# Layer 1 of a two-layer trunk: whole-block weight scaling and lower halves on GpSimd

## The chip, the cores and the metric

The kernel runs on one core of one Trainium2 chip. Its engines are PE (TensorE, matrix products), DVE (VectorE), ACT (ScalarE) and POOL (GpSimd); SP (SyncE) issues the transfers between HBM and SBUF, the on-chip memory. PSUM is the memory that PE writes its products to. Each engine works off its own queue in order and waits at semaphores for the others. The metric is the time of one execution on the device in microseconds (us). One execution was also recorded by the profiler; times inside it count from the span's start.

## The reference

A trunk of two layers over 1024 tokens of width 1024, in float32. Layer 0 is a native-sparse-attention mixer, layer 1 a "forgetting" attention, and each is followed by a gated ConvFFN. Only layer 1 matters here:

```python
h  = rms_norm(x, attn_norm[1])
hs = rms_norm(x, kv_norm) @ w_kv_shared            # keys, values, 12 forget gates
k_sh, v_sh = hs[..., :768], hs[..., 768:1536]      # 12 heads of 64 each
log_f = log_sigmoid(hs[..., 1536:] + b_fgate)
dcum  = cumsum(log_f, axis=1)
q, q_mem = h @ b_w_in[0]                           # 12 heads, 4 memory heads
s = q k^T / 8 + dcum[t] - dcum[s]                  # causal softmax, times v
x = x + concat(o_mix, o_mem) @ w_o[1]              # output projection
x = x + conv_ffn(rms_norm(x, ffn_norm[1]))
```

`rms_norm(x, g)` scales each of the 1024 columns by a factor of `g`. The kernel multiplies these factors into the weights: row d of a weight matrix is multiplied by g[d].

## The kernel before

Every float32 product is made of three matmuls: an operand is cut into an upper half (`hi`, rounded by a copy on ACT) and a lower half (`lo` = source minus `hi`, a subtraction), and `mm3` (L241 to L243) multiplies hi by hi, hi by lo and lo by hi. `split` (L162 to L169) makes the two halves: ACT copies at L165, and DVE subtracts at L166, or POOL, if `low` names it.

Layer 1 begins with the value projection and the forget gates: `layer1_v` fills PSUM tiles for 8 blocks of 128 tokens, in two passes of 390 columns, and its results `sv` are split on ACT and DVE and stored by SP. `forget` (L1386 and on) then takes the log-sigmoid of the 12 gates of all tokens, a tile `lsg` of 128x96: L1394 and L1395 on ACT, then a chain of 15 DVE instructions, L1396 to L1405, of which all but L1404 read what the one ahead of them wrote. PE waits for its result `r` at L1410, the matmul that starts the running sum, and stands still until it comes, because the matmuls of the second pass of `layer1_v` that follow are behind it in PE's queue.

After that `layer1_attn` runs `attention()`: the key and query projections (14 blocks of 128 output columns, in the order k0, q0, q6, k1, q1, k2, q2, q7, k3, q3, k4, q4, k5, q5) are filler between the steps of the attention units. Each block's weights are 128 partitions x 8 row groups x 128 columns. `proj` calls `load_block` with step 8, and that calls `load_rows` (L274 to L287): one transfer into a tile `wr` (three buffers), then for each of the 8 row groups one ACT instruction at L285 (upper half `wh`, 128x128, scaled by that group's factor `gc`) and one DVE instruction at L286 (lower half `wl` = `wr` times `gc` minus `wh`). `wh` and `wl` have four buffers each. Which instruction of the interleaved work comes where in an engine's queue is the scheduler's choice; a transfer into `wr` waits until the block that held the buffer has been read.

Towards the end of the attention `operand()` (L580 to L589) makes the 16 operands `hT` of the output projection: a transfer of two halves from HBM into `wr` (L587), their sum on POOL (L588), the upper half on ACT (L165) and the lower half on DVE (L166). Some are made while attention steps still run, the rest after the last one. The weights `w_o` of the output projection go through the same `wr` buffers (`load_rows` without factors, loads at L274). Other names below: `ps` are scores, normalised by DVE at L474 (a scaling from SBUF to SBUF); L518 makes the lower half of the transposed scores `pt` from PSUM; `st` are projected keys and queries.

Of the kernel before, what the change touches and what calls it, by code (L numbers as in the profile page):

```python
# [13 lines left out]
ALU = mybir.AluOpType  # L14
# [4 lines left out]
P = 128  # L19
# [3 lines left out]
KT = D // P  # L23
# [103 lines left out]
class Trunk:  # L127
# [422 lines left out]
    def attention(self, ap, l, od, units, work, spare, lead=4, lag=2, lead_work=2):  # L550
# [4 lines left out]
        steps, items, users = [], [], {}  # L555
# [23 lines left out]
        later, halves, whole, oT = {}, [], [], []  # L579

        def operand():

            if not oT:
                oT.extend(self.hpair() for _ in range(2))
            c, kt = whole.pop(0)
            raw = self.wraw([P, 2, CH])
            self.nc.sync.dma_start(raw, od[c][:, kt * P:(kt + 1) * P, :].rearrange("s p q -> p s q"))  # L587
            self.nc.gpsimd.tensor_tensor(raw[:, 0], raw[:, 0], raw[:, 1], ALU.add)  # L588
            self.split(raw[:, 0], oT[c][0][:, kt, :], oT[c][1][:, kt, :])  # L589

        def after(k, slot, f):
            later.setdefault((k, slot), []).append(f)
# [36 lines left out]
        for k in range(first, len(steps) + lag + 4):  # L629
            st = steps[k] if 0 <= k < len(steps) else None  # L630
            run(k, "max")
            if st:
                self.turn_p(ap, st)
                self.upper_p(ap, st)
            run(k, "exp")
            if st:
                self.lower_p(st)
            run(k, "norm")
            while items and items[0]["at"] <= k:
                begin(k, items.pop(0))  # L640
            if k < 0 and lead_work and items:
                for _ in range(lead_work):
                    if work:
                        advance()
            if st and k < n_fill:
                owed += max(total, 0) / (n_fill - k)
                while owed >= 1 and work:
                    owed -= 1
                    advance()
            if 0 <= k - lag < len(steps):  # L650
                for part in range(len(steps[k - lag]["t"])):
                    self.value(steps[k - lag], part)
                if steps[k - lag]["end"]:
                    finish(k, steps[k - lag]["u"])
            if not work and whole and k % 4 == 0:
                operand()
            if k == units[-1]["start"]:
                w_o = self.load_block(self.a["w_o"][l], [(0, CH)])
        while whole:
            operand()  # L660
# [769 lines left out]
    def layer1_attn(self, h, gc):  # L1430
        od = self.o_dram(1)
        wkv, wq = self.a["w_kv_shared"], self.a["b_w_in"][0]
        self.n_pt, self.n_q = 3, 1
        with self.tc.tile_pool(name="l1a", bufs=1) as ap:
            def proj(w, g, dst, m, scale):
                at = self.load_block(w, [(m * P, P)], g, 8)
                yield from self.plain_proj(ap, h, lambda kt: at(kt, 0, P), dst, m, scale)

            def k(m):
                return ("k", m), 9, proj(wkv, gc[:, 0:8], self.kd1, m, None)  # L1440

            def q(m):
                return ("q", m), 9, proj(wq, gc[:, 8:16], self.qd1, m, QSC)
            work = [k(0), q(0), q(6), k(1), q(1), k(2), q(2), q(7)]
            for m in range(3, 6):
                work += [k(m), q(m)]
            fox = list(self.units1(ap))
            mem = list(self.mem_units(ap, self.qd1[:, NH * HD:, :], self.mem[1], [("ps0", 1280, 2)] * 2, lambda h: ("q", 6 + h // 2), "dve"))
            units = []
            for i in range(6):  # L1450
                units += fox[4 * i:4 * i + 4] + (mem[2 * i:2 * i + 2] if i < 4 else [])
            return self.attention(ap, 1, od, units, work, 5)
# [521 lines left out]
```

## Time and profile before

| | us |
|---|---|
| median of 3 runs | 2570.05 (2568.84 to 2573.27) |
| the profiled execution | 2571.99 |
| its span, first to last instruction | 2570.2 |
| PE busy | 2465.7 (96%) |
| DVE busy | 1822.5 (71%) |
| ACT busy | 1339.1 (52%) |
| POOL busy | 794.5 (31%) |
| mean granted TensorE clock | 0.987 |

In the chain of work that ended last PE has 76% of the span, DVE 6%, ACT and DMA 4% each and POOL 3%. POOL does hardly anything in layer 1's attention: in the slices of the page from about 1400 to 1800 us its digit is 0. What counts is therefore where PE stands still in layer 1, and who ends that wait: the timelines list start, duration, engine, line and operation, and in square brackets how long the engine sat idle before and what released it.

### The profile page before, as it was taken

How to read it: one execution, taken by the hardware profiler on the slowest of the kernel's cores; microseconds unless marked ns; L12 is line 12 of the kernel's file. 1: busy time of each engine (PE TensorE's matmuls, PEld its weight loads, DVE VectorE, ACT ScalarE, POOL GpSimd, SP SyncE). 2: the span in 40 equal slices, each digit the busy share in tenths (PEclk: the TensorE clock that was granted, in tenths of full speed). 3: DMA queues.
4: the chain of work that ended last, by engine and by line, in shares of the span. 5: the costliest groups of instructions: out<-in, count | busy, mean ns of one | idle time of the engine just before them, and what ended most of it. 6: DMA issues, size and time to landing. Idle time of an engine off the chain costs nothing.

```text
span 2570.2 us, 35647 instructions
## 1 busy us (share of the span) xinstructions
PE 2465.7 (96%) x12306; PEld 2062.9 (80%) x12306; DVE 1822.5 (71%) x3074; ACT 1339.1 (52%) x2553; POOL 794.5 (31%) x714
## 2 busy tenths in 40 slices
PE   7889999988999999999999999999999999999998
PEld 7778888766778888888889988887777888888886
DVE  5638787676377778779665467878476777788765
ACT  5328787677145444444454356767234444445443
POOL 1335555476124554540000000000234555451000
PEclk9999999999999999999999999999999999999999
DMA  8473234243422332349334466665632233338533
GB/s 250 137 212 92 83 103 116 87 140 108 157 74 90 111 107 91 115 143 324 92 126 149 141 188 188 194 186 167 218 108 78 91 115 103 99 107 297 171 98 115
DMA packets 302700, 357.68 MB, mean 139 GB/s; under 512 B 37960, under 2 KB 183224, under 8 KB 302520
## 3 DMA queue, kind: packets, MB, share of 16 engines
q1 hardware_dynamic: 302520, 355.41, 44.1%
q8 instruction: 97, 1.59, 0.3%
q14 instruction: 83, 0.68, 0.1%
HBM read 245.55 MB, written 109.78 MB: 138 GB/s over the span
## 4 chain that ended last, share of the span: by engine, by line
PE 76%; DVE 6%; ACT 4%; DMA 4%; POOL 3%; issue 2%; SPq 0%; POOLq 0%; ACTq 0%; DVEq 0%
PE psa L241 12%; PE psa L242 12%; PE psa L243 12%; PE psb L241 9%; PE psb L243 9%; PE psb L242 9%; PE psa L384 5%; PE psb L504 4%; PE psb L528 4%; DVE pt L518 1%; ACT pt L515 1%; DVE ps L414 1%; ACT ps L427 1%; DMA wr<-o 1%; DMA wr<-in_w_up_dram 1%
## 5 line engine op out<-in xcount | busy, mean ns | idle before, releaser
L165 ACT ACTIVATE wh<-wr 128x512 fp32r<-128x512 f32 (+2 forms) x240 | 182.0, 760 | 314.1 <-PE psb L243 148.4
L1748 DVE SCALAR_TENSOR_TENSOR v<-u,cw,v 128x1023 f32<-128x1023 f32 (+1 forms) x176 | 273.1, 1552 | 68.8 <-ACT v L1746 68.5
L166 DVE TENSOR_TENSOR wl<-wr,wh 128x512 fp32r<-128x512 f32 (+2 forms) x232 | 223.2, 964 | 120.9 <-ACT wh L165 120.3
L518 DVE TENSOR_TENSOR pt<-psb,pt 128x512 fp32r<-128x512 f32 (+2 forms) x380 | 243.7, 659 | 71.3 <-ACT pt L515 69.7
L1746 ACT ACTIVATE v<-u,cw 128x1024 f32<-128x1024 f32 x88 | 109.6, 1246 | 309.9 <-DVE u L1735 283.2
L515 ACT ACTIVATE pt<-psb 128x512 fp32r<-128x512 f32 (+2 forms) x380 | 212.0, 575 | 111.7 <-PE psb L504 76.3
L528 PE MATMUL psb<-pt,vv 128*128 128x512 f32 (+2 forms) x864 | 245.5, 362 | 11.8 <-DVE pt L518 6.3
L241 PE MATMUL psa<-hT,wh 128*128 128x512 f32 x560 | 218.5, 391 | 5.3 <-DVE u L1709 5.3
L243 PE MATMUL psa<-hT,wl 128*128 128x512 f32 x560 | 218.3, 390 | 0.2 <-DVE wl L166 0.2
L242 PE MATMUL psa<-hT,wh 128*128 128x512 f32 x560 | 218.1, 390 | 0.0
L384 PE MATMUL psa<-kk,qq 128*128 128x512 f32 (+4 forms) x792 | 180.5, 347 | 23.9 <-DMA qq<-qd 12.4
L205 POOL TENSOR_TENSOR rs<-ss,consts 128x1 f32<-128x1 f32 x44 | 25.8, 588 | 573.2 <-DVE ss L203 400.7
L528 PEld LDWEIGHTS psb<-pt,vv 128*128 128x128 f32 x864 | 145.2, 191 | 33.5 <-DVE pt L518 11.9
L1650 POOL TENSOR_TENSOR ws<-wr 128x512 f32<-128x512 f32 x44 | 77.8, 1769 | 295.7 <-DMA wr<-in_w_up_dram 251.9
L414 DVE CUSTOM_DVE_ANT_0 ps<-psa,caub 128x128 f32<-128x128 f32 (+1 forms) x192 | 138.8, 750 | 41.1 <-PE psa L384 36.3
L427 ACT ACTIVATE ps<-ps,stat 128x128 f32<-128x128 f32 (+1 forms) x192 | 147.5, 771 | 30.9 <-DVE stat L414 30.7
L384 PEld LDWEIGHTS psa<-kk,qq 128*128 128x128 f32 x792 | 124.3, 195 | 45.5 <-issue 18.6
L241 PE MATMUL psb<-hT,wh 128*128 128x512 f32 x384 | 156.6, 408 | 1.1 <-ACT wh L165 0.9
L504 PE MATMUL psb<-consts,ps 128*128 128x128 f32 x928 | 149.4, 280 | 5.9 <-POOL ps L472 3.9
L243 PE MATMUL psb<-hT,wl 128*128 128x512 f32 x384 | 152.3, 397 | 0.8 <-POOL wl L166 0.6
L242 PE MATMUL psb<-hT,wh 128*128 128x512 f32 x384 | 151.2, 394 | 0.0
L588 POOL TENSOR_TENSOR wr<-wr 128x512 f32<-128x512 f32 x16 | 21.3, 1331 | 415.1 <-DMA kd<-st 248.0
(310 smaller groups left out, 6853.3 us busy)
## 6 DMA issues: line engine op xcount, KB each, us to landing
wr<-in_w_up_dram SPq DMA_DIRECT2D x88, 512.0 KB
wr<-gd SPq DMA_DIRECT2D x154, 256.0 KB
gd<-v SPq DMA_DIRECT2D x88, 256.0 KB
gd<-gs SPq DMA_DIRECT2D x66, 256.0 KB
o<-ob SPq DMA_DIRECT2D x128, 128.0 KB
wr<-o SPq DMA_DIRECT2D x32, 512.0 KB
hT<-in_w_down_dram SPq DMA_DIRECT2D x64, 256.0 KB
qd<-st SPq DMA_DIRECT2D x56, 256.0 KB
```

What stands on the lines that cost most here:

```text
L165: nc.scalar.activation(hi, src, AF.Copy)
L166: (low or nc.vector).tensor_tensor(lo, src, f32(hi), ALU.subtract)
L241: mm(out, lh, rh, start=first, stop=False, skip_group_check=more)
L242: mm(out, lh, rl, start=False, stop=False, skip_group_check=more)
L243: mm(out, ll, rh, start=False, stop=last, skip_group_check=more)
L384: nc.tensor.matmul(out, w, rhs, start=b not in banks[:i], stop=b not in banks[i + 1:])
L427: nc.scalar.activation(p, p, AF.Exp, bias=st[:, 0, ii:ii + 1], scale=-1.0, accum_out=st[:, 1, ii:ii + 1])
L504: nc.tensor.transpose(tp[0:kb, x:x + P], br["pt"][ii][:, o:o + kb], self.ident)
L515: self.nc.scalar.activation(st["hi"], st["src"], AF.Copy)
L518: self.nc.vector.tensor_tensor(st["lo"], st["src"], f32(st["hi"]), ALU.subtract)
L528: self.nc.tensor.matmul(u["o"][:, iis[0] * P:iis[0] * P + w], br["v"](j), t[:, x:x + w], start=st["begin"] and first and i == 0, stop=st[" ...
L1748: nc.vector.scalar_tensor_tensor(v[:, d:], u[:, :S - d], cw[:, tap, i:i + 1], v[:, d:], ALU.mult, ALU.add)
```

## The change

Two things in layer 1, and no others.

In `proj` the 14 weight blocks are no longer made by `load_rows`. POOL multiplies the whole block in place by the factors (one instruction of 128x1024, L1438 of the changed kernel), one ACT copy of 128x1024 makes the upper half (L165), and one POOL subtraction of 128x1024 the lower half (L166). So 112 ACT instructions become 14, and 112 DVE instructions become 28 on POOL.

In `operand()` the lower half of those operands that are made while attention steps still run (7 of the 16) moves from DVE to POOL.

```diff
@@ operand()
             self.nc.gpsimd.tensor_tensor(raw[:, 0], raw[:, 0], raw[:, 1], ALU.add)
-            self.split(raw[:, 0], oT[c][0][:, kt, :], oT[c][1][:, kt, :])
+            self.split(raw[:, 0], oT[c][0][:, kt, :], oT[c][1][:, kt, :], None, self.nc.gpsimd if k < len(steps) else None)
@@ layer1_attn()
             def proj(w, g, dst, m, scale):
-                at = self.load_block(w, [(m * P, P)], g, 8)
-                yield from self.plain_proj(ap, h, lambda kt: at(kt, 0, P), dst, m, scale)
+                raw = self.wraw([P, KT, P])
+                self.nc.sync.dma_start(raw, w[:, m * P:(m + 1) * P].rearrange("(k p) n -> p k n", p=P))
+                self.nc.gpsimd.tensor_tensor(raw, raw, g.rearrange("p (k o) -> p k o", o=1).to_broadcast([P, KT, P]), ALU.mult)
+                hi, lo = self.whl([P, KT, P])
+                self.split(raw, hi, lo, None, self.nc.gpsimd)
+                yield from self.plain_proj(ap, h, lambda kt: (hi[:, kt, :], lo[:, kt, :]), dst, m, scale)
```

The scheduler puts the instructions in another order with it. At the forget gates DVE had, before, the chain on `lsg` with one L286 of a weight block (`wl`) after nearly each step and a subtraction on `sv` at two places:

```order
L1396 TENSOR_SCALAR lsg<-lsg 128x96
L1397 RECIPROCAL lsg<-lsg 128x96
L166 TENSOR_TENSOR sv_2141_13373<-psb_13348,sv_2141_13373 128x6x64
L1398 TENSOR_TENSOR lsg<-lsg 128x96
L286 SCALAR_TENSOR_TENSOR wl_13871<-wr_13868,gc,wh_13870 128x128
L1399 TENSOR_TENSOR lsg<-lsg 128x96
L166 TENSOR_TENSOR sv_2141_13373<-psb_13348,sv_2141_13373 128x6
L1400 TENSOR_SCALAR lsg<-lsg 128x96
```

Now, on DVE at the same place:

```order
L1396 TENSOR_SCALAR lsg<-lsg 128x96
L1397 RECIPROCAL lsg<-lsg 128x96
L1398 TENSOR_TENSOR lsg<-lsg 128x96
L1399 TENSOR_TENSOR lsg<-lsg 128x96
L166 TENSOR_TENSOR sv_2141_13373<-psb_13348,sv_2141_13373 128x6x64
L1400 TENSOR_SCALAR lsg<-lsg 128x96
L1402 SCALAR_TENSOR_TENSOR lsg<-lsg 128x96
L166 TENSOR_TENSOR sv_2141_13373<-psb_13348,sv_2141_13373 128x6
L1402 SCALAR_TENSOR_TENSOR lsg<-lsg 128x96 x6
```

The weight instructions are gone from the chain, and the first `sv` subtraction stands two steps later in it.

ACT at the same place, now (`wh_13692`, `wh_13759` and `wh_13845` are the upper halves of k0, q0 and q6, `wh_13950` that of k1; before, single L285 stood between the others here, and the first `sv_2141` copy directly behind L1395):

```order
L165 ACTIVATE wh_13692<-wr_13689 128x1024
L165 ACTIVATE wh_13759<-wr_13756 128x1024
L165 ACTIVATE wh_13845<-wr_13842 128x1024
L165 ACTIVATE sv_2139_13319<-psb_13294 128x5x64
L165 ACTIVATE sv_2139_13319<-psb_13294 128x58
L1394 ACTIVATE lsg<-z 128x96
L1395 ACT_TABLE_LOAD
L1395 ACTIVATE lsg<-lsg 128x96
L165 ACTIVATE wh_13950<-wr_13947 128x1024
L165 ACTIVATE sv_2141_13373<-psb_13348 128x6x64
```

The copy of k1, which waits for POOL's multiplication of k1, now stands ahead of the `sv_2141` copy that the DVE queue waits for in the middle of the chain.

POOL's queue from the first weight block on, now (before, it had nothing between the sums of squares of the layer's norm and the first L588):

```order
L1438 TENSOR_TENSOR wr_13689<-wr_13689,gc 128x1024
L1438 TENSOR_TENSOR wr_13756<-wr_13756,gc 128x1024
L1438 TENSOR_TENSOR wr_13842<-wr_13842,gc 128x1024
L166 TENSOR_TENSOR wl_13693<-wr_13689,wh_13692 128x1024
L166 TENSOR_TENSOR wl_13760<-wr_13756,wh_13759 128x1024
L166 TENSOR_TENSOR wl_13846<-wr_13842,wh_13845 128x1024
L1438 TENSOR_TENSOR wr_13947<-wr_13947,gc 128x1024
L1438 TENSOR_TENSOR wr_14152<-wr_14152,gc 128x1024
L166 TENSOR_TENSOR wl_13951<-wr_13947,wh_13950 128x1024
L1438 TENSOR_TENSOR wr_14423<-wr_14423,gc 128x1024
L1438 TENSOR_TENSOR wr_14711<-wr_14711,gc 128x1024
L166 TENSOR_TENSOR wl_14156<-wr_14152,wh_14155 128x1024
```

The blocks are k0, q0, q6 (multiplied, then subtracted), then k1, q1, k2 and q2. Since `wr` has three buffers, the load of k1 waits for the subtraction of k0, that of q1 for the subtraction of q0, that of k2 for that of q6, and that of q2 for that of k1; SP's queue is in order, so what stands behind such a load waits with it.

At the end of the attention SP had, before, these transfers: an operand (`o` into `wr`, L587), then the four loads of the `w_o` weights, the third of which waits for a DVE instruction, the lower half of that operand:

```order
L587 DMA wr_17465<-o_1_13656 128x2x512 [waits DMAHW3_49]
L274 DMA wr_17482<-in_w_o_dram 128x2x512 [waits DMAHW4_49,DVE_49]
L274 DMA wr_17488<-in_w_o_dram 128x2x512 [waits DMAHW5_49,DVE_49]
L274 DMA wr_17494<-in_w_o_dram 128x2x512 [waits DMAHW3_49,DMAHW6_49,DVE_49,Activation_49]
L622 DMA o_1_13656<-ob_17457 64x512 [waits DMAHW7_49,Activation_49]
```

SP at the same place, now:

```order
L587 DMA wr_17283<-o_1_13656 128x2x512 [waits DMAHW3_49,Pool_49]
L274 DMA wr_17300<-in_w_o_dram 128x2x512 [waits DMAHW4_49,Pool_49]
L274 DMA wr_17306<-in_w_o_dram 128x2x512 [waits DMAHW5_49,Pool_49]
L274 DMA wr_17312<-in_w_o_dram 128x2x512 [waits DMAHW6_49,DMAHW3_49,Pool_49]
L274 DMA wr_17318<-in_w_o_dram 128x2x512 [waits DMAHW4_49,DMAHW7_49,DVE_49,Activation_49]
L622 DMA o_1_13656<-ob_17275 64x512 [waits DMAHW0_49,Activation_49]
```

Three loads now wait for POOL instead of DVE, and the fourth `w_o` load stands ahead of the store of an attention result (`ob`).

## Rows read from the trace of the kernel before

**Rows 1.** Windows: length, busy time and instructions of each engine, PEclk, DMA share, GB/s.

```profile
1420.00:1430.00 10.00, 8.14 (x46) 7.82 (x44) 8.66 (x36) 9.11 (x30) 0.00 (x0) 1.00 0.64 190
...
1460.00:1780.00 320.00, 316.33 (x1720) 265.62 (x1719) 238.70 (x594) 199.73 (x498) 5.55 (x5) 1.00 0.64 183
...
193.00:202.00 9.00, 7.92 (x28) 6.83 (x29) 4.73 (x26) 5.92 (x18) 2.64 (x3) 0.53 0.48 140
...
1431.00:1437.00 6.00, 6.00 (x21) 6.00 (x22) 2.23 (x12) 0.00 (x0) 0.00 (x0) 0.50 0.60 186
```

**Rows 2.** Waits of PE from 1380 to 1860 us: total, times, longest.

```profile
PE psb L528 <- DVE pt L518: 4.2, 8, 1.1
```

**Rows 3.** Timeline of PE: start, duration, operation, in brackets the idle time before.

```profile
1430.75 0.71 PE L1410 MATMUL psb<-lsg,tri 128*128 128x96 f32 x2 [2.60 <-issue]
...
1589.25 0.47 PE L241 MATMUL psb<-hT,wh 128*128 128x512 f32 x1
...
1830.50 0.50 PE L241 MATMUL psb<-wh,hT 128*128 128x512 f32 x1 [2.24 <-ACT hT L165]
```

**Rows 4.** Timeline of DVE in the forget gates.

```profile
1424.08 0.21 DVE L1396 TENSOR_SCALAR lsg<-lsg 128x96 f32<-128x96 f32 x1 [1.24 <-ACT lsg L1395]
1424.32 0.75 DVE L1397 RECIPROCAL lsg<-lsg 128x96 f32<-128x96 f32 x1
...
1425.40 0.25 DVE L1398 TENSOR_TENSOR lsg<-lsg 128x96 f32<-128x96 f32 x1
1425.57 0.35 DVE L286 SCALAR_TENSOR_TENSOR wl<-wr,gc,wh 128x128 fp32r<-128x128 f32 x1
...
1430.40 0.25 DVE L1405 SCALAR_TENSOR_TENSOR lsg<-lsg 128x96 f32<-128x96 f32 x1
```

**Rows 5.** Timelines of ACT and SP around the first weight blocks.

```profile
1408.55 1.13 ACT L285 ACTIVATE bh<-wr,gc 128x390 fp32r<-128x390 f32 x2 [0.48 <-DMA wr<-in_w_kv_shared_dram]
...
1423.95 0.47 ACT L165 ACTIVATE sv<-psb 128x384 fp32r<-128x384 f32 x1
...
1405.30 1.45 SPq L274 DMA_DIRECT2D wr<-in_w_kv_shared_dram  x2
...
1409.23 1.88 SPq L274 DMA_DIRECT2D wr<-in_b_w_in_dram  x2
```

**Rows 6.** Durations, by source line, by group (mean ns) and in ACT's timeline.

```profile
L286 DVE SCALAR_TENSOR_TENSOR wl<-wr,gc,wh x120: 317/344/883, 1374.2 to 1666.7; 128x128 fp32r<-128x128 f32 x112, 128x390 fp32r<-128x390 f32 x8
...
L1187 POOL TENSOR_TENSOR wl<-wr,wh x2: 2392/2402/2411, 168.2 to 358.0; 128x1024 fp32r<-128x1024 f32 x2
...
L470 POOL TENSOR_TENSOR pm<-pm,stat 128x1024 f32<-128x1024 f32 x8 | 15.2, 1896 | 0.3
...
1791.67 1.05 ACT L165 ACTIVATE wh<-wr 128x1024 fp32r<-128x1024 f32 x1
```

**Rows 7.** Timelines of DVE and POOL where the two meet, and once where they don't.

```profile
1642.87 1.29 POOL L588 TENSOR_TENSOR wr<-wr 128x512 f32<-128x512 f32 x1 [247.98 <-DMA kd<-st]
...
1643.43 1.15 DVE L286 SCALAR_TENSOR_TENSOR wl<-wr,gc,wh 128x128 fp32r<-128x128 f32 x2
...
1789.69 1.29 POOL L588 TENSOR_TENSOR wr<-wr 128x512 f32<-128x512 f32 x1 [8.75 <-DMA wr<-o]
...
1789.77 2.29 DVE L474 TENSOR_SCALAR ps<-ps,stat 128x128 f32<-128x128 f32 x4
...
1571.17 1.27 DVE L474 TENSOR_SCALAR ps<-ps,stat 128x128 f32<-128x128 f32 x4
...
1572.95 0.86 DVE L286 SCALAR_TENSOR_TENSOR wl<-wr,gc,wh 128x128 fp32r<-128x128 f32 x3
```

**Rows 8.** The end of the attention: SP's waits (1780 to 1835 us), ACT, DVE.

```profile
SPq L274 <- DVE hT L166: 8.5, 1, 8.5
...
1791.15 0.62 ACT L165 ACTIVATE hT<-wr 128x512 fp32r<-128x512 f32 x1
...
1797.39 0.68 DVE L166 TENSOR_TENSOR hT<-wr,hT 128x512 fp32r<-128x512 f32 x1
```

## The prediction

> **What bounds the kernel now.** I read the windows first. From 1460 to 1780 us, where the attention and the 14 projections run, PE is busy 316.33 of 320 us [rows 1]. Whatever DVE and ACT are relieved of there, at most the 3.7 us in which PE stands still can come back. So the change can move the time only where PE waits, and I looked for these places in PE's waits and in its timeline. Three matter. At 1430.75 PE has stood still for 2.60 us before L1410 [rows 3]; the profile names no releaser, but L1410 reads the `r` that the chain on `lsg` makes, and that chain ends on DVE at 1430.40 plus 0.25 us [rows 4], just before PE starts. Then PE waits for lower halves of `pt` from DVE, 4.2 us in eight pieces [rows 2]. Last, an operand of the output projection comes 2.24 us late at 1830.50 [rows 3]. The gap at L1410 has a second cost: right after it the granted clock is 0.50 for 6 us with PE busy throughout [rows 1], the lower of its two levels (1.2 GHz), where it was 1.00 before. Six us of work at half speed are some 3 us lost.
>
> **Part 1: weights in the forget gates (1420 to 1440 us).** What goes: in the chain, nearly every L1402 is followed by an L286 of 0.35 us [rows 4], nine in all. Without them a step takes its own 0.25 us instead of some 0.43. Nine times about 0.2 is 1.7 us earlier, if nothing else changes.
>
> What comes: POOL's queue. A whole-block multiplication has no row with these operands; the nearest is the broadcast multiplication L470 of the same shape, 1.90 us. The subtraction has an exact row, 2.40 us, and ACT's whole copy takes 1.05 us [rows 6]. Next, when POOL can start. The loads of q0 and q6 are issued from 1409.23 on, the second by 1411.1 [rows 5]. A load issued at 1405.30 released ACT at 1408.55, 3.3 us later [rows 5]; three blocks in a row share the bandwidth, so I estimate q6 in SBUF between 1414 and 1416. POOL then finishes multiplying q6 at 1415.9 to 1418.0, and the three subtractions (7.2 us) at 1423.1 to 1425.2. I take the later, since the blocks are loaded together. Then follow, in the queue's order: multiply k1 to 1427.2, multiply q1 to 1429.2, subtract k1 to 1431.7, multiply k2 to 1433.7, and multiply q2, whose load is issued only after k1's subtraction and so lands at 1435 at the earliest.
>
> Before, POOL did nothing here [rows 1]; the chain had never to share anything with it. What such a meeting costs is seen later in the trace. At 1643.43 two L286 take 1.15 us, and the longest one of all is 0.88 instead of 0.34 us [rows 6, 7]; POOL's L588 runs from 1642.87 to 1644.16, so that the DVE instruction ends just after POOL's. At 1789.77 four L474 take 2.29 us, against 1.27 elsewhere; they begin 0.08 us after a POOL instruction of 1.29 us [rows 7]. The DVE instruction did not run slower, it stood until POOL was through. Two kinds are hit: one with two inputs in SBUF, and a scaling from SBUF to SBUF. The chain on `lsg` is made of these two kinds, L1397 aside. The Trainium skill has this as a rule (page "SBUF — State Buffer", section "Who interferes with whom"): VectorE with two SBUF inputs, or in a two-port mode, and GpSimd exclude each other for the whole instruction, whichever starts first. By that rule the chain's 96-column steps are blocked as the 128-column ones of the rows were, and the sum is the one below; without it, it would be the lower end. The rows agree with it.
>
> So I walk the chain: each step waits for the POOL instruction that has started, and POOL takes its next one before the next step is ready. L1396 ends at about 1425.4, L1397 runs beside the multiplication of k1, L1398 ends at 1427.4, L1399 at 1429.4, L1400 at 1431.9, the first L1402 at 1433.9. Then POOL waits for q2's load, and nine steps of 0.25 us follow: `r` at 1436.3 instead of 1430.65, **5.6 us later**. A second wait lies inside this: ACT's copy of k1 waits for the multiplication of k1 (1427.2), ends at 1428.25, and only then does ACT do the `sv` copy that it did at 1423.95 [rows 5]; DVE's subtraction on it now stands ahead of L1400, so DVE cannot go on before 1428.8. If POOL blocked nothing, ten steps of 0.25 us and two `sv` subtractions would follow, `r` at 1431.9: **+1.2 us**, the lower end. The upper end is a multiplication as slow as the subtraction (2.40): four of them end the last blocked step 2 us later, **+7.6**. I take 5.6, because L470 has the change's operation and shape.
>
> The Trainium skill (page "GPSIMD Engine Reference", section 4.1) speaks against such a move altogether: element-wise work of two inputs belongs on VectorE, GpSimd being about twice as slow. Our rows have 2.40 on POOL against eight L286 of 0.34 (2.8 us) on DVE for a block, so here it is no slower for the block; by the page alone POOL's multiplication would also stand near the upper end, and the sum 2 us higher.
>
> The clock: after a gap of 12.4 us at 181 to 194 us, 193 to 202 shows 0.53 [rows 1], so a longer gap costs some 4 us against the 3 of now. I put 0 to +0.8, and take 0.
>
> **Part 2: the other blocks (1460 to 1780 us).** DVE loses 80 L286 of 0.35 us there, 28 us, and ACT about as much; PE gets next to nothing of it, as said. A block now needs 1.90 + 1.05 + 2.40 = 5.4 us in a row, where L285 and L286 overlapped. That would hurt PE only if a block came in the nick of time. It doesn't: the eighth block's last L286 ends at 1573.8 [rows 7], and PE reads the block at 1589.25 [rows 3], 15 us later; it is the tightest one of those I looked at. Against DVE's relief stands the blocking: some 29 new POOL instructions of about 2 us, each holding up an L474 with some chance; half a us to 0.7 each makes 15 to 20 us. Both nearly cancel on an engine that isn't the bound: **0**, with −3 (all of PE's standing still) and +3 (as many lower halves of `pt` late again) as ends.
>
> **Part 3: the end of the attention (1780 to 1832 us).** SP waits 8.5 us with the third `w_o` load for the lower half of an operand [rows 8]. Its upper half is done by 1791.8, but DVE comes to it only at 1797.39, because scores and `pt` stand ahead of it [rows 8]. On POOL it takes about the 1.29 us of the addition of the same shape [rows 7] and ends at 1793.1, 5 us sooner. The loads behind it on SP go out sooner, the last operands come 2 to 5 us earlier, and of the 2.24 us at 1830.50 most should go: **−2.5**. At best also the half-us waits around it and some of the waits for `pt`, −6; at worst the DVE order, which now has two lower halves of `w_o` ahead of a `pt` that PE needs, gives back 2 us more than it wins, +2.
>
> **Sum**: 5.6 + 0 + 0 − 2.5 = +3.1 us. The profiled execution (2571.99) is 1.9 above the median of 2570.05, with 1.8 us outside its span of 2570.2. I put the +3.1 on the median: **2573.1 us**, and a profile near 2575.
>
> **Rivals.**
> - *Faster: the chain goes free.* POOL is through with its six instructions by 1423.1, multiplies k1 by 1425.0, the `sv` copy is done at 1426.5, and nothing blocks steps of 96 columns. Then `r` comes at about 1429.5, the gap is 1.4 us, and the clock stays up: −1.2 − 3, with part 3 −2.5, or −6.7: 2563. Against it stand the two meetings of rows 7. 0.18.
> - *Slower: POOL never runs dry.* The whole price hangs on whether q2's load lands before POOL is done with k2's multiplication, 1433.7. If so, POOL goes on with multiply q2 and the subtractions of q1, k2 and q2, 9.1 us, and holds up four more of the nine last steps: `r` near 1443.5, +12.8, with part 3 and the clock +10.5: 2580. My estimate has the load 1.3 us too late for that, less than the uncertainty of POOL's start. 0.29.
> - *A block comes late for PE* (or the attention's `pt` chain does, blocked by POOL): the 5.4 us of a block against 15 us of slack. If it came to that, 5 to 8 us in all: 2577. 0.05.
>
> **How the numbers follow.** My forecast has 0.48. About 0.2%, 5.1 us, is what a measurement of this kernel tells from no change. Of the forecast, 0.42 lies within it (up to 2575.2), 0.05 above and 0.01 below. With the rivals: faster 0.19, same 0.42, slower 0.39. The forecast's own range is 2568 to 2578. For 8 in 10 the range takes in part of both outer cases: 2564 to 2580.
>
> **What would show it.** In the new trace: `r` (L1405) at 1436 and PE's wait before L1410 at about 8 us; steps L1396 to L1402 each ending just behind a POOL instruction; POOL's L1438 at 1.9 us and its subtraction at 2.4; a stretch at 0.5 of the clock after the gap, about as long as now; PE busy as before from 1460 to 1780; SP's 8.5 us at the `w_o` load mostly gone. The prediction is wrong if the steps keep their 0.25 us beside POOL, if POOL is still multiplying and subtracting when the last L1402 runs, or if PE's wait for `pt` grows.

## Result and profile after

The change makes the kernel slower by half a per cent. The prediction (2573.1 us, range 2564 to 2580) was too low.

| | before | changed |
|---|---|---|
| median of 6 runs, us | 2571.19 (2568.84 to 2573.27) | 2583.1 (2581.08 to 2584.96) |
| ratio, 95% interval | | 1.0051 (1.0039 to 1.0062) |
| the profiled execution, us | 2571.99 | 2584.96 |
| its span, us | 2570.2 | 2583.0 |
| mean granted clock | 0.987 | 0.989 |

To see where the 13 us arise I compare when the same matmul starts in both profiles (the n-th matmul of a line; columns: its time before, cells: how much later it starts now, both counted from the span's start).

| at, us before | 1420 | 1460 | 1551 | 1690 | 1764 | 2550 |
|---|---|---|---|---|---|---|
| changed | −0.6 | +3.9 | +4.2 | +12.2 | +11.5 | +12.8 |

So 4.5 us arise at the forget gates, 8.0 between 1551 and 1690, and 1.3 from 1764 to the end. The windows of the changed kernel follow (columns as in [rows 1]). The third is as long as 1460 to 1780 before and begins with the same work, but 45 fewer matmuls fit into it; the fourth is the same work as 1551 to 1690 before:

```profile
1420.00:1430.00 10.00, 7.57 (x43) 7.24 (x41) 6.25 (x10) 4.14 (x8) 9.76 (x6) 1.00 0.69 200
1431.00:1437.00 6.00, 1.20 (x5) 1.23 (x6) 4.45 (x12) 0.00 (x0) 3.33 (x3) 0.65 0.31 88
1464.00:1784.00 320.00, 311.51 (x1675) 260.67 (x1675) 219.12 (x498) 182.77 (x418) 47.58 (x25) 0.99 0.63 180
1555.00:1702.00 147.00, 139.60 (x761) 116.69 (x760) 111.17 (x250) 90.66 (x208) 31.39 (x15) 0.99 0.64 182
```

and the last one of before:

```profile
1551.00:1690.00 139.00, 136.68 (x761) 115.11 (x761) 116.69 (x306) 98.92 (x258) 1.29 (x1) 1.00 0.67 192
```

The same 761 matmuls took 139 us and take 147. DVE is busy 5.5 us less and ACT 8.3 us less, as the change meant; PE stands still 7.4 us instead of 2.3, and its busy time is 2.9 us longer; some 1.8 of these are a stretch at the lower clock (0.91 on the mean from 1620 to 1640, where before had 1.00). PE's waits from 1380 to 1870 us in the changed kernel, against [rows 2]:

```profile
PE psb L1410 <- issue: 8.2, 1, 8.2
PE psb L528 <- DVE pt L518: 5.3, 11, 1.0
PE psb L528 <- ACT pt L515: 2.9, 4, 1.2
...
PE psb L504 <- DVE pt L518: 2.2, 3, 1.2
...
PE psb L504 <- DVE ps L474: 1.2, 2, 1.0
```

and two of them before:

```profile
PE psb L528 <- ACT pt L515: 0.8, 3, 0.4
...
PE psb L504 <- DVE pt L518: 0.2, 1, 0.2
```

**The forget gates.** DVE and POOL in the changed kernel, to be read beside [rows 4]:

```profile
1422.55 0.27 DVE L1396 TENSOR_SCALAR lsg<-lsg 128x96 f32<-128x96 f32 x1 [1.95 <-ACT lsg L1395]
...
1423.64 1.59 DVE L1398 TENSOR_TENSOR lsg<-lsg 128x96 f32<-128x96 f32 x1
1425.27 1.84 DVE L1399 TENSOR_TENSOR lsg<-lsg 128x96 f32<-128x96 f32 x1
...
1429.22 2.31 DVE L1402 SCALAR_TENSOR_TENSOR lsg<-lsg 128x96 f32<-128x96 f32 x1
...
1435.44 0.26 DVE L1405 SCALAR_TENSOR_TENSOR lsg<-lsg 128x96 f32<-128x96 f32 x1
```

```profile
1417.99 7.13 POOL L166 TENSOR_TENSOR wl<-wr,wh 128x1024 fp32r<-128x1024 f32 x3
1425.08 1.91 POOL L1438 TENSOR_TENSOR wr<-wr,gc 128x1024 f32<-128x1024 f32 x1
1427.23 1.90 POOL L1438 TENSOR_TENSOR wr<-wr,gc 128x1024 f32<-128x1024 f32 x1 [0.24 <-DMA wr<-in_b_w_in_dram]
1429.08 2.34 POOL L166 TENSOR_TENSOR wl<-wr,wh 128x1024 fp32r<-128x1024 f32 x1
1431.38 1.91 POOL L1438 TENSOR_TENSOR wr<-wr,gc 128x1024 f32<-128x1024 f32 x1
1435.96 1.90 POOL L1438 TENSOR_TENSOR wr<-wr,gc 128x1024 f32<-128x1024 f32 x1 [2.67 <-DMA wr<-in_b_w_in_dram]
```

Each of the slow steps ends 0.1 to 0.15 us behind a POOL instruction: L1398 at 1425.23 behind the third subtraction (1425.12), L1399 at 1427.11 behind the multiplication of k1 (1426.99), L1402 at 1431.53 behind the subtraction of k1 (1431.42). Between 1427.1 and 1428.5 DVE waits for the `sv` copy that ACT does behind its copy of k1.

**Between 1550 and 1690.** Here it is the normalisation of the scores: L442 guards the row sums against zero and L474 scales the scores `ps`; PE then transposes them (L504), ACT and DVE make the halves of `pt` from that (L515, L518), and PE multiplies `pt` by the values (L528). L442 takes 0.17 us in every one of its 32 places before, and L474 at most 1.30. In the changed kernel (DVE, four places, and POOL at the first two):

```profile
1562.61 2.51 DVE L474 TENSOR_SCALAR ps<-ps,stat 128x128 f32<-128x128 f32 x1
...
1591.65 4.47 DVE L474 TENSOR_SCALAR ps<-ps,stat 128x640 f32<-128x640 f32 x4
...
1625.45 1.40 DVE L442 TENSOR_SCALAR stat<-stat 128x4 f32<-128x4 f32 x1
...
1628.10 2.42 DVE L474 TENSOR_SCALAR ps<-ps,stat 128x128 f32<-128x128 f32 x4
...
1562.63 2.40 POOL L166 TENSOR_TENSOR wl<-wr,wh 128x1024 fp32r<-128x1024 f32 x1 [1.17 <-ACT wh L165]
...
1592.35 2.62 POOL L166 TENSOR_TENSOR wl<-wr,wh 128x1024 fp32r<-128x1024 f32 x1 [1.17 <-ACT wh L165]
```

A row names the shape of its first instruction. Four L474, from 128x128 on, took 1.27 us undisturbed [rows 7]; here the first alone takes 2.51. Four from 128x640 on took 2.33 before and take 4.47, and four columns of factors (L442, 128x4) take 1.40. From 1460 to 1680 all L442 and L474 together are 8.6 us longer than their undisturbed durations. PE waits for what comes behind them: 1.21 us for `pt` just after the 4.47 us. A wait of 1.72 us that ends at 1654.41 has another door: the profile names a load of `qq`, but ACT's copy of `pt` ends at 1654.35, just before it. ACT had stood 3.59 us for POOL's multiplication of k5 (1.9 us of it the multiplication; until 1649.86 POOL itself waited for the block's load), and with it the `pt` copies:

```profile
1596.78 0.44 PE L504 MATMUL psb<-consts,ps 128*128 128x128 f32 x2 [1.21 <-DVE pt L518]
```

```profile
1651.79 1.06 ACT L165 ACTIVATE wh<-wr 128x1024 fp32r<-128x1024 f32 x1 [3.59 <-POOL wr L1438]
```

### The profile page after: what moved, and what is told of

The parts are those of the page before. It is cut to its first block, busy times and chain, and to the rows that moved or that the text cites. A ratio compares the mean times of both kernels' runs of the same rounds, so it can differ in the third digit from the quotient of the medians.

```text
span 2583.0 us, 35482 instructions
## 1 busy us (share of the span) xinstructions
PE 2462.2 (95%) x12306; PEld 2057.1 (80%) x12306; DVE 1813.9 (70%) x2955; ACT 1322.6 (51%) x2455; POOL 858.2 (33%) x749
## 4 chain that ended last, share of the span: by engine, by line
PE 75%; DVE 6%; ACT 4%; DMA 4%; issue 3%; POOL 3%; SPq 1%; POOLq 0%; ACTq 0%; DVEq 0%
PE psa L241 12%; PE psa L242 11%; PE psa L243 11%; PE psb L241 9%; PE psb L243 9%; PE psb L242 9%; PE psa L384 5%; PE psb L504 4%; PE psb L528 4%; DVE pt L518 1%; ACT pt L515 1%; DVE ps L414 1%; DVE wl L166 1%; DMA wr<-o 1%; DMA wr<-in_w_up_dram 1%
## 5 line engine op out<-in xcount | busy, mean ns | idle before, releaser
L165 ACT ACTIVATE wh<-wr 128x512 fp32r<-128x512 f32 (+2 forms) x254 | 196.9, 777 | 329.2 <-PE psb L243 146.1
L166 DVE TENSOR_TENSOR wl<-wr,wh 128x512 fp32r<-128x512 f32 (+2 forms) x232 | 223.3, 964 | 119.3 <-ACT wh L165 118.7
L518 DVE TENSOR_TENSOR pt<-psb,pt 128x512 fp32r<-128x512 f32 (+2 forms) x380 | 243.8, 659 | 84.4 <-ACT pt L515 82.8
L515 ACT ACTIVATE pt<-psb 128x512 fp32r<-128x512 f32 (+2 forms) x380 | 211.8, 575 | 121.1 <-PE psb L504 85.1
L528 PE MATMUL psb<-pt,vv 128*128 128x512 f32 (+2 forms) x864 | 243.1, 360 | 16.8 <-DVE pt L518 7.2
L528 PEld LDWEIGHTS psb<-pt,vv 128*128 128x128 f32 x864 | 143.6, 189 | 39.8 <-ACT pt L515 12.4
L504 PE MATMUL psb<-consts,ps 128*128 128x128 f32 x928 | 148.6, 279 | 8.5 <-POOL ps L472 3.5
L241 PE MATMUL psa<-hx,wh 128*128 128x512 f32 x368 | 144.0, 392 | 0.5 <-ACT u L1742 0.5
```

The source lines that it names most:

```text
L165: nc.scalar.activation(hi, src, AF.Copy)
L166: (low or nc.vector).tensor_tensor(lo, src, f32(hi), ALU.subtract)
L241: mm(out, lh, rh, start=first, stop=False, skip_group_check=more)
L504: nc.tensor.transpose(tp[0:kb, x:x + P], br["pt"][ii][:, o:o + kb], self.ident)
L515: self.nc.scalar.activation(st["hi"], st["src"], AF.Copy)
L518: self.nc.vector.tensor_tensor(st["lo"], st["src"], f32(st["hi"]), ALU.subtract)
```

## Experiments

Two theories. **A**: POOL's instructions hold DVE's up, in both places, and the chains that PE waits for run through those DVE instructions. **B**: it is the longer way of a block (transfer, multiplication, copy, subtraction), above all ACT waiting for a multiplication. All comparisons are with runs of the kernel before on the same chip; single executions of it spread over some 14 us (2561.42 to 2575.39), so medians and intervals count. The table of delays gives one profiled execution each, and what is read there is only the change from one column to the next. The edits below are shortened: `(g broadcast)` stands for the factors as in the change, and lines that only move are left out.

| | ratio to before, 95% | 1420 | 1460 | 1551 | 1690 | 1764 | 2550 |
|---|---|---|---|---|---|---|---|
| e1 first seven blocks on POOL | 1.0022 (1.0011 to 1.0033) | −2.4 | +2.5 | +2.7 | +4.7 | +4.5 | +1.9 |
| e2 upper half not behind POOL | 1.0066 (1.0052 to 1.0080) | +1.5 | +8.7 | +8.8 | +16.9 | +17.2 | +17.7 |
| e3 both weight steps on DVE | 1.0015 (1.0005 to 1.0025) | −2.1 | +1.8 | +1.8 | +1.5 | +1.5 | +2.1 |
| e4 operands alone | 0.9992 (0.9983 to 1.0001) | +0.9 | −1.9 | −1.9 | −2.7 | −2.7 | −2.8 |
| e5 idle work on POOL | 1.0098 (1.0084 to 1.0112) | −3.4 | −5.1 | +0.2 | +16.8 | +20.1 | +21.1 |
| e6 POOL in pieces | 1.0092 (1.0077 to 1.0107) | −2.3 | +6.0 | +6.2 | +23.0 | +22.3 | +21.5 |
| e7 changed, gates covered | 1.0021 (1.0010 to 1.0031) | +0.5 | −1.6 | −1.5 | +7.0 | +6.8 | +7.0 |
| e8 operands alone, gates covered | 0.9986 (0.9976 to 0.9997) | −5.2 | −11.0 | −11.1 | −8.4 | −8.6 | −11.1 |
| e9 last seven blocks on POOL | 1.0010 (1.0000 to 1.0020) | −1.8 | −4.6 | −4.6 | +1.0 | +0.2 | −2.1 |
| e10 before, gates covered | 0.9992 (0.9982 to 1.0002) | +0.5 | −5.3 | −5.4 | −3.5 | −3.7 | −1.4 |
| e11 POOL only writing | 1.0022 (1.0011 to 1.0032) | +1.3 | −1.9 | +1.6 | +5.8 | +6.1 | +8.6 |
| e12 weights on DVE, gates covered | 0.9985 (0.9976 to 0.9993) | +2.3 | −3.5 | −3.6 | −3.0 | −3.0 | −4.6 |

### The two places one by one: e1 and e9

```diff
 def proj(w, g, dst, m, scale):
+    if not (m < 3 or (m == 6 and scale is not None)):   # e1; e9 without "not"
+        at = self.load_block(w, [(m * P, P)], g, 8)
+        yield from self.plain_proj(ap, h, lambda kt: at(kt, 0, P), dst, m, scale)
+        return
```

> The operand change as in the changed kernel, but only the first seven weight blocks (k0, q0, q6, k1, q1, k2, q2, those at and around the forget gates) are made on POOL; the other seven as before. Theory: the loss of the changed kernel (12 to 13 us) has two places, some 4.5 us at the forget gates (gap of 8.2 us before L1410) and 8 us between 1550 and 1670 us, where the later blocks are made. Then this kernel keeps the first and loses the second: +4 to +6 us against before, PE's wait before L1410 still about 8 us. Rival (the later loss is a consequence of the first delay, for example other orders of transfers after it): +10 us or more.

> The counterpart of e1_first7_new: the first seven weight blocks as before on ACT and DVE, only the last seven (q7, k3, q3, k4, q4, k5, q5) on POOL; the operands as in the changed kernel. Theory: PE's wait before L1410 is the 2.6 us of before, the 8 us between 1550 and 1670 us stay; +6 to +9 us. Rival (the later loss needs the delay at the forget gates ahead of it): +3 us or less.

e1 came out as theory said: PE's wait before L1410 is 8.5 us, 4.9 us are lost up to 1460 and 2.0 between 1551 and 1690. e9 has PE's wait of 2.6 us as before and loses 5.6 us between 1551 and 1690; the later blocks need no delay ahead of them to do harm. But it is only 0.10% slower than before, 0 to 5 us by the interval, and not the 6 to 9 us that I expected; by that figure alone the rival (3 us or less) would have it, and it is the profile that speaks against it. Part of the shortfall may be the operand change (below). And some 1.8 of the 8.0 us were the slow clock of 1620 to 1640, which e9's execution does not have (its clock is 1.00 from 1546 to 1691). The two ratios add up to 0.32%, the change has 0.51%. Both kernels carry the operand change; with e4's −0.08% counted once and not twice the sum is 0.40%. Each ratio is uncertain by 0.1%, and whether the rest is chance or an interplay stays open.

### ACT's wait or DVE's: e2 and e3

```diff
 e2, in proj of the changed kernel
+    for k in range(KT):
+        self.nc.scalar.activation(hi[:, k, :], raw[:, k, :], AF.Identity, scale=g[:, k:k + 1])
     self.nc.gpsimd.tensor_tensor(raw, raw, (g broadcast), ALU.mult)
-    self.split(raw, hi, lo, None, self.nc.gpsimd)
+    self.nc.gpsimd.tensor_tensor(lo, raw, f32(hi), ALU.subtract)
 e3
-    self.nc.gpsimd.tensor_tensor(raw, raw, (g broadcast), ALU.mult)
-    self.split(raw, hi, lo, None, self.nc.gpsimd)
+    self.nc.vector.tensor_tensor(raw, raw, (g broadcast), ALU.mult)
+    self.split(raw, hi, lo)
```

> The changed kernel, but ACT makes the upper half from the unscaled block with eight instructions and the factor as scale, as before; POOL then multiplies in place and subtracts, as in the changed kernel. So ACT never waits for POOL's multiplication (6.4 us of such waits between 1550 and 1690 us in the changed kernel), while POOL's instructions still stand beside DVE's. Theory A (DVE is held up by POOL's instructions, the order of ACT's queue matters little): the 8 us of 1550 to 1670 us stay, at least 6 of them; in all +9 to +13 us against before. Rival B (ACT's queue standing behind the multiplication is what delays pt and PE): at least half of the 8 us goes, +5 to +8 us in all.

> The changed kernel with both whole-block instructions of the weights (multiplication and subtraction, 128x1024) on DVE instead of POOL; the operands as in the changed kernel. Theory A (POOL's instructions holding DVE up are the cause in both places): no such meeting is left except at the operands, the chain on lsg waits at most for whole DVE instructions that the scheduler puts into it (1.2 us each); -2 to +4 us against before. Rival (whole blocks as such, with the longer way from transfer to weight and ACT waiting for a multiplication, are the cause): +6 us or more.

With ACT freed of the wait, the loss between 1551 and 1690 stays (8.1 us) and the whole is worse, +0.66%: beyond what theory A gave (13 us), and far from B. POOL's two instructions now follow each other directly, and the L474 get longer still:

```profile
1640.45 5.09 DVE L474 TENSOR_SCALAR ps<-ps,stat 128x128 f32<-128x128 f32 x4
...
1640.44 1.90 POOL L1441 TENSOR_TENSOR wr<-wr,gc 128x1024 f32<-128x1024 f32 x1 [3.60 <-ACT wh L1440]
1642.42 2.52 POOL L1442 TENSOR_TENSOR wl<-wr,wh 128x1024 fp32r<-128x1024 f32 x1
```

Four L474 stand through both POOL instructions, 1.27 us of work in 5.09. With the same whole blocks on DVE (e3) the loss between 1551 and 1690 is gone (−0.3), though ACT still waits for a multiplication and a block still goes the same three steps. That is B's end as the main cause. What is left of e3 sits at the forget gates, where the scheduler puts whole blocks into the chain; PE's wait there, and one such instruction in the chain:

```profile
PE psb L1410 <- issue: 6.9, 1, 6.9
```

```profile
1426.38 1.22 DVE L1438 TENSOR_TENSOR wr<-wr,gc 128x1024 f32<-128x1024 f32 x1
```

### POOL's work without its results: e5 and e11

```diff
 e5, in proj; raw, hi and lo as before on ACT and DVE
+    jk = self.sb(ap, [P, KT, P], F32, "jk", 1)
+    self.nc.gpsimd.tensor_tensor(jk, raw, (g broadcast), ALU.mult)      # ahead of ACT's
 ...
+    self.nc.gpsimd.tensor_tensor(jk, jk, f32(hi), ALU.subtract)         # behind DVE's
 e11: each of the two replaced by one column of it and
+    for _ in range(2):
+        self.nc.gpsimd.memset(jk, 0.0)
```

> The kernel before (weights made by ACT and DVE, operands with DVE), with two added POOL instructions for each weight block that nobody needs: a multiplication of the loaded block into a spare tile and a subtraction of the upper half in that tile, 128x1024 both, as long and at about the same times as those of the changed kernel. Nothing on DVE, ACT or PE waits for them; only the buffer of the load is held longer. Theory A (POOL's instructions hold DVE's up): the loss of the changed kernel comes without its dependencies, PE's wait before L1410 at 6 us or more, 6 us or more lost between 1550 and 1670 us; +9 us or more in all. Rival (weights come late because POOL makes them, or ACT waits for POOL): +4 us or less.

> As e5_pool_beside, but POOL's added instructions read next to nothing: for each of the two a product or difference of one column (it keeps the place and the waits) and two memsets of the spare tile, 128x1024. If POOL holds DVE up only by reading SBUF: at most 3 us slower than before. If writing is enough to hold up the scalings from SBUF to SBUF (L474, L442, L1396) but not the instructions with two SBUF inputs (L286, L1402): part of e5's loss, +4 to +12 us, the L474 lengthened and the L286 not. If any POOL instruction holds up both: as e5, +15 us or more (less as the memsets are shorter).

e5 is direct evidence for A: no engine waits for a result of the added instructions, and the kernel becomes 1% slower, 16.6 us of it between 1551 and 1690. The loads, whose buffers POOL now reads too, do come later: k1's is issued at 1485 us instead of 1419, and PE once waits 1.5 us for a `wl`. But e11, whose loads are as late (k1's at 1488), loses only 4.2 us in that stretch. The part of the expectation on the forget gates was not tested: the first added instruction waits until 1460 us for the last stores of `sv`, presumably because the spare tile takes their place in SBUF, and PE's wait before L1410 is 2.3 us. Since DVE still had its own L286 here (L1443), these were held up too. The same place in e5 and in e11, six instructions of 128x128 with two inputs in SBUF, POOL beside them reading in the first and only writing in the second:

```profile
1583.79 3.81 DVE L1443 SCALAR_TENSOR_TENSOR wl<-wr,gc,wh 128x128 fp32r<-128x128 f32 x6
...
1584.50 2.42 POOL L1444 TENSOR_TENSOR jk<-jk,wh 128x1024 f32<-128x1024 f32 x1 [3.89 <-ACT wh L1442]
```

```profile
1585.10 1.66 DVE L1445 SCALAR_TENSOR_TENSOR wl<-wr,gc,wh 128x128 fp32r<-128x128 f32 x6
...
1597.83 0.69 DVE L442 TENSOR_SCALAR stat<-stat 128x4 f32<-128x4 f32 x1 [1.41 <-ACT ps L424]
...
1584.03 1.97 POOL L1448 MEMSET jk<- 128x1024 f32 x2
...
1596.53 1.96 POOL L1448 MEMSET jk<- 128x1024 f32 x2
```

3.81 us beside a subtraction of 2.42, 1.66 where four of the six meet the second of two memsets. But the scaling L442 (usually 0.17) takes 0.69 and ends with the memsets. So writing alone holds up the scalings from SBUF to SBUF, and the instructions with two SBUF inputs only give way to a POOL that reads. Between 1460 and 1680 none of the L1445 that met a memset was longer than usual (0.35 at most). One later one takes 0.97 us beside a memset (at 1738.55); right ahead of it in DVE's queue an L442 takes 1.04, and both end at 1739.52 with the memset, so it may have stood behind that one. This was not tested. The whole is +0.22%, at the lower end of the middle case. This is what the Trainium skill states (page "SBUF — State Buffer", section "Who interferes with whom"): two SBUF inputs conflict with a GpSimd instruction that reads and not with one that only writes; for the two-port modes, which copies and scalings can enter, it has no such limit. The runs agree with it, 3.81 against 1.66 us.

### Shorter pieces: e6

```diff
-    self.nc.gpsimd.tensor_tensor(raw, raw, (g broadcast), ALU.mult)
+    for k in range(KT):
+        self.nc.gpsimd.tensor_tensor(raw[:, k, :], raw[:, k, :], g[:, k:k + 1].to_broadcast([P, P]), ALU.mult)
     hi, lo = self.whl([P, KT, P])
-    self.split(raw, hi, lo, None, self.nc.gpsimd)
+    self.nc.scalar.activation(hi, raw, AF.Copy)
+    for k in range(KT):
+        self.nc.gpsimd.tensor_tensor(lo[:, k, :], raw[:, k, :], f32(hi[:, k, :]), ALU.subtract)
```

> The changed kernel with each of POOL's two weight instructions cut into eight of 128x128 (one row group each), so that POOL does the same work in the same order but lets go after about 0.3 us each (128x256 takes 0.65 us on POOL in the trace of before). Theory A: a DVE instruction waits for one piece at most; PE's wait before L1410 falls to 3 to 6 us, the loss between 1550 and 1670 us to 3 us or less, +2 to +7 us in all. Rival (what counts is that a block's way through POOL takes 4 us and more, whatever the size of an instruction): +11 us or more.

My expectation failed: +0.92%, nearly double the changed kernel's loss. By the figure it is the rival's, by the trace it is neither. POOL needs longer in pieces (one every 0.37 and 0.42 us, so some 2.9 and 3.4 us a block instead of 1.90 and 2.40), but above all three scalings on DVE did not get in between two pieces. Two of them, and PE's wait behind the second:

```profile
1422.59 5.70 DVE L1396 TENSOR_SCALAR lsg<-lsg 128x96 f32<-128x96 f32 x1 [1.95 <-ACT lsg L1395]
...
1433.75 2.53 DVE L1402 SCALAR_TENSOR_TENSOR lsg<-lsg 128x96 f32<-128x96 f32 x6
...
1628.02 8.05 DVE L442 TENSOR_SCALAR stat<-stat 128x4 f32<-128x4 f32 x1
...
1637.67 0.47 PE L504 MATMUL psb<-consts,ps 128*128 128x128 f32 x1 [6.55 <-DVE ps L474]
```

```profile
1418.08 10.05 POOL L1443 TENSOR_TENSOR wl<-wr,wh 128x128 fp32r<-128x128 f32 x24
1428.09 5.50 POOL L1439 TENSOR_TENSOR wr<-wr,gc 128x128 f32<-128x128 f32 x15
...
1623.66 5.79 POOL L1439 TENSOR_TENSOR wr<-wr,gc 128x128 f32<-128x128 f32 x16
1629.39 6.65 POOL L1443 TENSOR_TENSOR wl<-wr,wh 128x128 fp32r<-128x128 f32 x16
```

L1396 stands until the 24 subtractions are through (1428.13; it ends 1428.29), and a scaling of four columns stands 8.05 us, until POOL's last piece. The third, an L442 at 1665.03, stands 2.97 us. PE's wait before L1410 is 11.8 us instead of 8.2; with the 6.55 us this is 10 of the 12.5 us that e6 loses more than the changed kernel from 1420 to 1690.

Most scalings did get in, however. Of the 14 that met POOL's pieces in the attention and at the gates, 11 waited for the running piece at most, such as these within one unbroken row of multiplications:

```profile
1592.35 0.19 DVE L442 TENSOR_SCALAR stat<-stat 128x4 f32<-128x4 f32 x1 [0.71 <-ACT ps L427]
...
1592.98 2.82 DVE L474 TENSOR_SCALAR ps<-ps,stat 128x640 f32<-128x640 f32 x4
...
1592.11 4.30 POOL L1439 TENSOR_TENSOR wr<-wr,gc 128x128 f32<-128x128 f32 x8 [22.97 <-DMA wr<-in_w_kv_shared_dram]
```

The four L474 usually take 2.33 us, the row of POOL 2.91. The L1402, with two SBUF inputs, get one turn per piece (0.42 us each). So for a scaling the length of one POOL instruction is no bound on the wait; it can stand for POOL's whole unbroken row. What decides whether it does, no run shows.

### The gates' wait covered: e7, e8, e10 and e12

```diff
 for t in range(NT):
-    if t % 2 == 0:
+    if t in (0, 4, 6):
         next(forget, None)
     self.layer1_v(vp, h, 1, t, w1, self.psb()[:, 0:390], fb, z)
```

> The changed kernel with one number changed: the running sum of the forget gates (L1410, L1411) stands behind four blocks of the second value pass in PE's queue instead of two, the transposes behind six instead of four. PE then has some 8.5 us more of other work while DVE makes the chain. Theory: PE's wait before L1410 (8.2 us) goes almost wholly and the slow clock behind it too, the 8 us later stay: -8 to -10 us against the changed kernel, +2 to +5 against before. Rival (the delay only moves, to the first projections or the first attention units, which need the gates' sums): no better than +9.

> The kernel before with the operand change and the same change of order as e7_after_cover. Theory: the wait of 2.6 us before L1410 goes, and with it the slow clock that some executions show behind it (3 us); -3 to -7 us against before. Rival (PE finds the same wait elsewhere): within 2 us of before.

> The kernel before with the change of order of e7 and e8 alone (running sum of the gates behind four blocks of the second value pass). The difference to e8_operand_cover is the operand change, with no wait and no slow clock at the forget gates that could differ. Prediction's part 3: this kernel is 2 us or more slower than e8. Theory from the traces: within 1.5 us of e8, so -2 to -5 us against before.

> e3_dve_whole (both whole-block instructions of the weights on DVE, operands as in the changed kernel) with the order of e7 and e8. If the loss of the changed kernel is POOL's instructions beside DVE's, and the wait at the forget gates is covered by the order, nothing of it is left: -2 to -6 us against before, like e8_operand_cover (-3.6 us as measured). If whole blocks as such cost something (DVE away for 1.2 us at a time, ACT waiting for a multiplication): 0 or slower.

The running sum now stands behind four blocks of value matmuls, so that PE has other work while DVE makes the chain. In e7 PE's wait before L1410 is gone (1.3 us of others are left behind it), and from 1420 to 1460 us the delay goes from +0.5 to −1.6 instead of from −0.6 to +3.9, so 6.6 us come back; the 8.5 us between 1551 and 1690 stay, as theory said (+0.21%, 5.4 us by the ratio, 7.0 by the medians, at and above the upper end of what I expected). Not all of them are POOL's: with the same order and no weights on POOL, e10 loses 1.9 us and e8 2.7 us there, so some 6 are left, near e9's 5.6. This is e1's and e9's statement by another way: two places, and neither needs the other. In e8 PE does not stand still at all in the gates' place, and the clock stays at its upper level (2.4 GHz):

```profile
1430.00:1450.00 20.00, 20.00 (x118) 19.76 (x117) 6.56 (x22) 3.51 (x10) 0.00 (x0) 1.00 0.37 108
```

e8 and e12 are faster than before by 0.14% and 0.15% (3.6 and 3.9 us), and so beat both kernels: the first with the operand change and the weights as they were, the second with the operand change and whole weight blocks on DVE. e10, the new order alone, is at 0.9992 (0.9982 to 1.0002), not clear of no change. e12 differs from e7 in one thing, the engine of the two weight steps, and it loses next to nothing between 1551 and 1690 (+0.6): with the gates covered the change's idea of whole blocks was harmless, its engine was not.

### The operands alone: e4

```diff
-    self.split(raw[:, 0], oT[c][0][:, kt, :], oT[c][1][:, kt, :])
+    self.split(raw[:, 0], oT[c][0][:, kt, :], oT[c][1][:, kt, :], None, self.nc.gpsimd if k < len(steps) else None)
```

> Only the operand change: the lower half of seven operands on POOL, weights as before. The prediction gave this part -2.5 us (-6 to +2). Reading both traces, PE's delay against before is the same at the start and at the end of the last 50 us of the attention within 1.3 us, so the theory now is 0 to +1.5 us. Rival (the prediction's part 3 was right and its gain is eaten by other delays of the changed kernel): -2 us or better.

0.9992 (0.9983 to 1.0001), −2.0 us, not clear of no change; e8 against e10, which differ in the same edit, gives −0.06% or 1.5 us, with overlapping intervals. Both point to the prediction's −2.5 rather than to my theory of 0 to +1.5, and neither proves it. e4's profile also shows how chance enters: its wait before L1410 is the 2.6 us of [rows 3], but the clock stays up behind it, where [rows 1] had 0.50:

```profile
1431.00:1437.00 6.00, 5.33 (x31) 5.36 (x32) 3.15 (x16) 0.27 (x1) 0.00 (x0) 1.00 0.74 228
```

## Why the prediction was wrong

**Part 1, the forget gates: right.** The step-by-step walk gave a wait of about 8 us before L1410, 5.6 us more than before; it is 8.2, and 5.6 more. POOL's durations were as taken (1.90 and 2.34 to 2.40), the chain's steps end behind POOL's instructions, and POOL ran dry before the multiplication of q2 (it starts at 1435.96, after L1405 at 1435.44), so the "slower" rival did not come. Single steps met other POOL instructions than in the walk: L1396 ended 2.6 us earlier than walked, so L1398 already stood behind the third subtraction, L1400 was not held up, and two L1402 were instead of one. That did not matter, because k2's multiplication sets the end (walked 1433.7, measured 1433.29). `r` comes 5.05 us later by the span's time; the rest of the 5.6 is PE reaching the gap 0.6 us earlier, which was chance. The clock's part was put at 0 to +0.8 and is −1.1: the slow stretch began within the gap, so less of it fell on work.

**Part 2, the other blocks: this step failed.** The prediction put it at 0, with ±3 as ends, and it is +8.0 in the changed kernel's profile, 5.6 in e9's. It had the mechanism, and even too much of it (15 to 20 us of blocked DVE time, against the 8.6 us measured on L442 and L474), but it set that against the 28 us of work that DVE was relieved of, and called the sum nothing because DVE isn't the bound. That is the error: the relief is throughput on an engine with slack, which PE never waited for, while the blocking is delay in the short chain from the scores over L442, L474 and L518 to the next matmul, where hold-ups of up to 2.2 us each come through: 8.6 us of them became 8.0 us of PE's time in the changed kernel, 8.5 became 5.6 in e9, and 11.7 became 8.1 in e2. The upper end of 3 us was taken from how long PE waits for `pt` before; nothing bounded it there. The slow clock behind the new waits (some 1.8 us) and the wait behind ACT were not in the sum at all (ACT's copy standing 3.59 us for a load and POOL's multiplication), nor that the L474 of a unit stand in a row, so that one POOL instruction hits all that follow.

The price of one meeting was not the fault. [rows 7] has four L474 taking 1.0 us longer beside a POOL instruction of 1.29 us, the prediction put in 0.5 to 0.7 us for each POOL instruction, and the 8.6 us over the 17 weight instructions of POOL between 1460 and 1680 are some 0.5 each. What was missing was to follow such a row of L474 on to the matmul that waits behind it, as was done for the chain on `lsg` in part 1.

**Part 3, the end of the attention: about right alone, nothing in the whole.** e4 and e8 against e10 allow the −2.5. In the changed kernel SP's wait at the third `w_o` load fell from 8.5 to 3.5 us, but DVE's lower halves of `w_o` took its place:

```profile
SPq L274 <- DVE wl L166: 3.8, 1, 3.8
SPq L274 <- POOL hT L166: 3.5, 1, 3.5
```

From 1764 us to the end the delay grows from 11.5 to 12.8 us; the prediction's upper end for it was +2. The clock hides part of this: over the same matmuls (1764 to 1862 before, 1775.5 to 1873.9 now) PE stands still 12.3 us instead of 9.1, but the mean clock is 0.98 instead of 0.95.

**Sum.** 5.6 − 1.1 + 8.0, and 0.9 for all the rest, are the 13.4 us between the first and the last column of the changed kernel; the prediction had 5.6 + 0 + 0 − 2.5. Besides, the kernel before has a median of 2571.19 us over six runs, 1.1 above the 2570.05 of three on which the prediction stood. The prediction's chance of 0.39 for slower, its second rival (2580) and the "waits of `pt`" rival (2577, at 0.05) lay on the right side; the last was the right kind and was priced too low and held too unlikely.

## What to carry to other kernels

Before work is moved to GpSimd, list the VectorE instructions that it will run beside, and sort out those that read two inputs from SBUF or scale from SBUF to SBUF: these can stand until GpSimd's instruction is through, a scaling sometimes for its whole unbroken row, and the price is paid by the chains that they belong to, not by VectorE's busy share. Relief of an engine with slack was worth nothing here against delay in a chain that the bounding engine waits for, so the two should not be set off against each other. A wait that a long chain causes can be covered by giving the waiting engine other work first, as one changed number did here (+0.21% instead of +0.51%).

## What the runs showed of the hardware that I had not expected

- GpSimd instructions that follow each other without a wait can keep a VectorE scaling from SBUF to SBUF out for the whole row: 8.05 us for 128x4, 5.70 us for 128x96, with pieces of only 0.40 to 0.47 us. They need not: 11 of 14 such scalings in e6 got in after one piece at most. VectorE instructions with two SBUF inputs got a turn after each piece (0.42 us a step).
- A reciprocal from SBUF to SBUF was not held up: L1397 takes 0.75 us beside POOL's subtraction, as before without it.
- A GpSimd memset, which only writes, holds up the scalings (0.69 instead of 0.17 us) but not the instructions with two SBUF inputs (1.66 us for six, four of them beside a memset, against 3.81 beside a subtraction).
- The same wait of 2.6 us of TensorE was followed by some 6 us at 1.2 GHz in one execution and by none in another of the same order of work (0.50 and 1.00 in the same stretch).
